# Gate and up tiles of three SwiGLU sublayers by seven half-size block products

## The chip, the core and the metric

One core of a Trainium2 chip runs the whole program. The metric is the device time of one execution in microseconds (us). TensorE (PE) multiplies; VectorE (DVE), ScalarE (ACT) and GpSimd (POOL) do the rest; SyncE (SP) issues the loads.

## The reference, cut to what matters

Two layers over 256 latent tokens and 256 context tokens with 1024 features. Each layer is an FFN sublayer, a mixer (a gated convolution in the first layer, windowed attention in the second) and another FFN sublayer. Each sublayer's input is normed and modulated by adaLN coefficients, which are products of silu(c) with a large projection w_mod.

```
def swiglu(h, w_gu, w_down):
    gu = h @ w_gu
    return (jax.nn.silu(gu[..., :D_FF]) * gu[..., D_FF:]) @ w_down

def ffn_sublayer(x, mod, k, g_pre, g_post, w_gu, w_down):
    h = adaln_in(x, g_pre, mod[k], mod[k + 1])
    return adaln_out(x, swiglu(h, w_gu, w_down), g_post, mod[k + 2], HALF_STEP)
```

D_FF is 2816, so w_gu has 22 feature tiles of 128 for the gate and 22 for up, each over 8 contraction tiles. Three FFN sublayers serve both token streams with the same weights; the fourth serves the latent stream alone.

## The kernel before

Everything lies with the features on the partitions: a stream is 8 tiles of 128 features by 512 tokens, the latent 256 (slice X) in front of the context 256 (slice Z). A float32 product is three float32r products: each operand is split into a high and a low part, and high x high, low x high and high x low are summed in PSUM (groups(), lines 398 to 400).

Weights come in slots of eight 128x128 tiles (512 KB). load() fetches a slot into a ring of RAW = 3 raw buffers, ACT writes its high part (line 243) and DVE, or POOL for the slots listed in POOL, its low part (line 244), into rings of RING = 8 buffers each. All loads are issued by SP in one order.

An FFN sublayer, ffn(l, j), is named by 3 * l + j: 0, 2 and 3 are the ones the change touches. Its 22 feature tiles go in three chunks (CHUNKS). A chunk first makes silu(gate) * up for its tiles, then multiplies them with the chunk's part of w_down into y, tile by tile of the output (project()). A tile of gate/up is one gate_up(): 48 matmuls of 512 columns, a silu on ACT (line 436), a product out of PSUM on DVE (line 438), and the split of the result (lines 408 and 409). In sublayers 2 and 3 the first four tiles are taken twice, for X and then for Z with 256 columns, so that the norms of the sublayer before can run beside them (HEADS, norms(), AT_HEAD); the end of a sublayer is halved in the same way (TAIL). In sublayer 0 the first two tiles run with the start.

Between these jobs pace() puts the adaLN sums: a step fetches one tile of w_mod (line 267) and takes the row sums of the one fetched before with silu(c), one DVE instruction per stream, called a dot here (line 297). NMODS says how many of the 18 chunks of eight steps are done by the end of sublayer 0, of the conv mixer and of sublayer 2; the rest go into sublayer 3. The last four chunks serve the latent stream alone.

The order of PE's instructions is that of the program. The other engines' order is made by a scheduler, except that instructions marked by keep() stay in the program's order. PSUM has four banks for products (bank()).

Of the kernel before, what the change touches and what calls it, by code (L numbers as in the profile page):

```python
# [18 lines left out]
F32 = mybir.dt.float32  # L19
# [13 lines left out]
CHUNKS = {0: ((0, 7), (7, 14), (14, 22)), 2: ((0, 7), (7, 14), (14, 22)), 3: ((0, 7), (7, 14), (14, 22))}  # L33
# [5 lines left out]
# feature tiles of the first two adaLN chunks: by dots, by pairs; and the loads ahead of the first product (latent  # L39
# and context stream, tiles for dots, tiles of pairs, weights)  # L40
# [4 lines left out]
RAW = 3  # L45
# [5 lines left out]
NMODS = (7, 6, 15)  # L51
# [15 lines left out]
# order in which the adaLN chunks are worked out: (layer, chunk, also for the context stream)  # L67
# [24 lines left out]
def halves_of(w):
    """[K, 1024] -> [K / 128, 128, 1024]: rows of two K tiles per slot, the front half of the columns first"""
    k = w.shape[0] // P
    return w.reshape(k // 2, 2, P, 2, 512).transpose(3, 0, 2, 1, 4).reshape(k, P, D)


def ffn_slots(w_gu, w_down, chunks):
# [3 lines left out]
    for a, b in chunks:  # L102
        out.append(slots_of(np.stack([gu[a:b], gu[FT + a:FT + b]], 1).reshape(-1, P, P)))
        out.append(slots_of(dn[:, a:b].reshape(-1, P, P)))
# [3 lines left out]
def lay_out(i):  # L108
    f = np.float32
    w = []  # L110
    w += ffn_slots(i["ffn_w_gu"][0, 0], i["ffn_w_down"][0, 0], CHUNKS[0])
    # the products of the first four slots run together, contraction tile by tile
# [4 lines left out]
    w += ffn_slots(i["ffn_w_gu"][0, 1], i["ffn_w_down"][0, 1], CHUNKS[2])  # L117
    w += ffn_slots(i["ffn_w_gu"][1, 0], i["ffn_w_down"][1, 0], CHUNKS[3])
# [6 lines left out]
    # the last sublayer keeps all of silu(gate) * up; its output comes with the tokens on the partitions  # L125
# [7 lines left out]
    # the first two chunks are taken together. Some of their feature tiles are worked out as the other chunks are;  # L133
    # the others go through the tensor engine, by pairs, with the rows of the projection on the partitions
# [10 lines left out]
    # constants of the shapes  # L145
# [26 lines left out]
# (half of the features, columns of it)  # L172
# [3 lines left out]
class Kernel:  # L176
    def __init__(self, ctx, tc, a):
# [40 lines left out]
        # silu(c), silu(c_ctx): on every partition, and with the features on the partitions  # L218
# [12 lines left out]
    # ---- streams of weights  # L231
    def load(self):
# [37 lines left out]
    def mod_step(self, last=False):  # L270
        """fetch one 128-feature tile of the adaLN projections, work out the one fetched before"""
# [22 lines left out]
    def dot(self, wt, v, b, out):  # L294
        """out = b + row sums of wt * silu(c)"""
# [3 lines left out]
    def keep(self, inst):  # L299
        """leave the marked instructions of an engine in the order of the program"""  # L300
# [24 lines left out]
    def spread(self, prb, r):  # L325
        """the same on all partitions, tokens along the row (PSUM)"""
# [7 lines left out]
    def new_h(self):  # L334
        """tiles of the modulated normed stream that the next product reads"""
# [41 lines left out]
    def weave(works, chain=None, at=()):  # L377
        """emit the works' products; the steps of chain go between them, at the given times (us of products)"""
# [41 lines left out]
    def gate_up(self, sl, base, ms, act):  # L420
        """silu(gate) * up of the feature tiles ms, whose products run together"""
# [11 lines left out]
        for i, m in enumerate(ms):  # L433
            pg, pu = banks[2 * i:2 * i + 2]
            sg = self.wk.tile([P, N], F32, name="sg", tag="tmp", bufs=3)
            nc.scalar.activation(sg[:, :n], pg[:, :n], AF.Silu)  # L436
            pr = self.wk.tile([P, N], F32, name="pr", tag="tmp", bufs=3)
            self.keep(nc.vector.tensor_mul(pr[:, :n], pu[:, :n], sg[:, :n]))  # L438
            self.hilo(act[m], sl, pr[:, :n], keep=True)

    def project(self, sl, base, ms, nk, act, y, part, fin=None):
        """y[m] (+)= W[:, m]^T act, for all of ms together; finished tiles are squared into the sums of fin and given
        their coefficients"""
# [651 lines left out]
```

## Time and profile before

| | us |
|---|---|
| median of 3 runs | 1680.61 |
| lowest and highest of the runs | 1678.48, 1683.15 |
| span of the profiled execution | 1676.8 |
| PE busy | 1642.4 |
| DVE busy | 1048.6 |
| ACT busy | 644.0 |
| POOL busy | 265.3 |

The profiled execution has no time of its own beside its span; the median of the runs lies 3.8 us above that. The span runs from the first to the last instruction. Busy times of different engines overlap. Matmuls are pipelined, so the time that one is shown with is longer than the step from one to the next; the step is read by counting matmuls in a stretch without waits.

### The profile page before, as it was taken

How to read it: one execution, taken by the hardware profiler on the slowest of the kernel's cores; microseconds unless marked ns; L12 is line 12 of the kernel's file. 1: busy time of each engine (PE TensorE's matmuls, PEld its weight loads, DVE VectorE, ACT ScalarE, POOL GpSimd, SP SyncE). 2: the span in 40 equal slices, each digit the busy share in tenths (PEclk: the TensorE clock that was granted, in tenths of full speed). 3: DMA queues.
4: the chain of work that ended last, by engine and by line, in shares of the span. 5: the costliest groups of instructions: out<-in, count | busy, mean ns of one | idle time of the engine just before them, and what ended most of it. 6: DMA issues, size and time to landing. Idle time of an engine off the chain costs nothing.

```text
span 1676.8 us, 23525 instructions
## 1 busy us (share of the span) xinstructions
PE 1642.4 (98%) x9378; PEld 1419.1 (85%) x9378; DVE 1048.6 (63%) x1570; ACT 644.0 (38%) x1051; POOL 265.3 (16%) x192
## 2 busy tenths in 40 slices
PE   8999999999999999999999999999999999989998
PEld 3788888889988998888888998888888997889987
DVE  7779779856644375977965564344443679665553
ACT  4532322325432643322232543222222558654442
POOL 1100000125102430000110521000000664130000
PEclk9999999999999999999999999999999999999999
DMA  8557556543322224655655224444433221045551
GB/s 317 188 164 237 189 187 217 194 156 102 101 89 101 68 71 165 213 188 165 219 191 166 80 74 148 160 132 150 153 124 114 94 89 64 26 160 198 194 192 50
DMA packets 70306, 246.73 MB, mean 147 GB/s; under 512 B 7730, under 2 KB 10290, under 8 KB 70196
## 3 DMA queue, kind: packets, MB, share of 16 engines
q1 hardware_dynamic: 69908, 245.02, 44.3%
q8 instruction: 73, 1.20, 0.3%
q14 instruction: 37, 0.30, 0.1%
q10 hardware_dynamic: 288, 0.20, 0.0%
HBM read 244.15 MB, written 1.05 MB: 146 GB/s over the span
## 4 chain that ended last, share of the span: by engine, by line
PE 90%; DVE 5%; ACT 2%; POOL 1%; issue 1%; DMA 1%; SPq 0%; DVEq 0%; POOLq 0%; ACTq 0%
PE mm L399 27%; PE mm L398 27%; PE mm L400 27%; PE mm L925 1%; PE mm L926 1%; PE mm L924 1%; PE po L801 1%; DVE junk L297 1%; PE tp L787 1%; POOL acc L359 1%; PE mm L747 1%; DMA xr<-in_xz 1%; PE prb L318 0%; ACT whi L243 0%; DVE acc L360 0%
## 5 line engine op out<-in xcount | busy, mean ns | idle before, releaser
L398 PE MATMUL mm<-hh,whi 128*128 128x512 f32 (+1 forms) x1520 | 549.3, 361 | 4.3 <-ACT hh L408 4.0
L399 PE MATMUL mm<-hh,wlo 128*128 128x512 f32 (+1 forms) x1520 | 547.9, 360 | 0.0
L400 PE MATMUL mm<-hl,whi 128*128 128x512 f32 (+1 forms) x1520 | 543.1, 357 | 0.0
L243 ACT ACTIVATE whi<-raw 128x1024 fp32r<-128x1024 f32 x316 | 330.5, 1056 | 440.2 <-PE mm L400 372.4
L244 DVE TENSOR_TENSOR wlo<-raw,whi 128x1024 fp32r<-128x1024 f32 x260 | 325.8, 1261 | 203.3 <-ACT whi L243 202.2
L398 PEld LDWEIGHTS mm<-hh,whi 128*128 128x128 f32 x1520 | 285.8, 188 | 53.6 <-ACT hh L408 5.3
L400 PEld LDWEIGHTS mm<-hl,whi 128*128 128x128 f32 x1520 | 285.9, 188 | 45.0 <-DVE hl L409 0.6
L399 PEld LDWEIGHTS mm<-hh,wlo 128*128 128x128 f32 x1520 | 286.3, 188 | 41.3
L297 DVE CUSTOM_DVE_ANT_0 junk<-wmd,sc,vec 128x1024 bf16<-128x1024 f32 x232 | 304.7, 1313 | 17.0 <-DMA wmd<-in_wmd 13.2
L244 POOL TENSOR_TENSOR wlo<-raw,whi 128x1024 fp32r<-128x1024 f32 x56 | 140.1, 2507 | 1005.2 <-ACT whi L243 1001.5
L398 PE MATMUL mm<-ah,whi 128*128 128x256 f32 (+1 forms) x848 | 276.8, 326 | 0.0
L399 PE MATMUL mm<-ah,wlo 128*128 128x256 f32 (+1 forms) x848 | 276.0, 326 | 0.0
L400 PE MATMUL mm<-al,whi 128*128 128x256 f32 (+1 forms) x848 | 274.1, 323 | 0.0
L398 PEld LDWEIGHTS mm<-ah,whi 128*128 128x128 f32 x848 | 160.5, 189 | 14.9
L400 PEld LDWEIGHTS mm<-al,whi 128*128 128x128 f32 x848 | 160.5, 189 | 14.1
L399 PEld LDWEIGHTS mm<-ah,wlo 128*128 128x128 f32 x848 | 160.8, 190 | 12.7
L438 DVE TENSOR_TENSOR pr<-mm,sg 128x512 f32<-128x512 f32 (+1 forms) x96 | 56.1, 584 | 181.6 <-PE mm L400 127.5
L436 ACT ACTIVATE sg<-mm 128x512 f32<-128x512 f32 (+1 forms) x96 | 49.2, 513 | 301.7 <-PE mm L400 301.7
L399 PE MATMUL mm<-h,wlo 128*128 128x256 f32 x352 | 98.8, 281 | 0.0
L398 PE MATMUL mm<-h,whi 128*128 128x256 f32 x352 | 98.6, 280 | 0.0
L400 PE MATMUL mm<-h,whi 128*128 128x256 f32 x352 | 98.4, 280 | 0.0
L409 DVE TENSOR_TENSOR al<-pr,ah 128x512 fp32r<-128x512 f32 (+1 forms) x84 | 74.6, 888 | 13.3 <-ACT ah L408 13.2
(185 smaller groups left out, 1496.5 us busy)
## 6 DMA issues: line engine op xcount, KB each, us to landing
raw<-in_wst SPq DMA_DIRECT2D x316, 512.0 KB, 3.5
wmd<-in_wmd SPq DMA_DIRECT2D x140, 512.0 KB, 4.2
xr<-in_xz SPq DMA_DIRECT2D x2, 1024.0 KB, 9.8
wmq<-in_wmd SPq DMA_DIRECT2D x8, 256.0 KB, 7.8
out_y<-xt SPq DMA_DIRECT2D x3, 256.0 KB, 2.1
rtab<-in_cst SPq DMA_DIRECT2D x1, 512.0 KB, 3.6
out_y<-xt SPq DMA_DIRECT2D x2, 128.0 KB, 1.8
msk<-in_cst ACTq DMA_DIRECT2D x1, 192.0 KB, 4.0
```

The costliest lines, as they stand in the source:

```text
L243: nc.scalar.activation(hi, raw, AF.Copy)
L244: d = sub.tensor_tensor(lo, raw, hi.bitcast(F32), ALU.subtract)
L297: self.keep(self.nc.vector.tensor_tensor_reduce(junk, wt, self.sc[v], 1.0, b, ALU.mult, ALU.add, out))
L359: nc.gpsimd.tensor_tensor(acc, acc, sq, ALU.add)
L398: nc.tensor.matmul(pt[:, :n], whi, rhi[:, sl], start=i == 0, stop=False)
L399: nc.tensor.matmul(pt[:, :n], wlo, rhi[:, sl], start=False, stop=False)
L400: nc.tensor.matmul(pt[:, :n], whi, rlo[:, sl], start=False, stop=i == last)
L409: i = (sub or self.nc.vector).tensor_tensor(lo[:, sl], src, hi[:, sl].bitcast(F32), ALU.subtract)
L436: nc.scalar.activation(sg[:, :n], pg[:, :n], AF.Silu)
L438: self.keep(nc.vector.tensor_mul(pr[:, :n], pu[:, :n], sg[:, :n]))
L747: nc.tensor.matmul(sp[e], act[4 * p2 + 2 * jp + jj][x][rows[e], qs], kt[p2][w][rows[e], :], start=a == 0, stop=False)
L787: nc.tensor.transpose(tp[:, c * P:(c + 1) * P], pe[c][:, kc // 2, kc % 2 * P:(kc % 2 + 1) * P], self.ident)
```

## The change

In sublayers 0, 2 and 3 the gate/up tiles from number SEVEN (6, 4 and 4) on are taken in pairs. The product of two feature tiles of gate and up with all 512 tokens is seen as a 2 x 2 block product: the weights in four blocks a11 (up, front half of the contraction), a21 (gate, front), a22 (gate, back) and a12 (up, back), each one slot; the input h in four blocks by the halves of the contraction and the two streams. Seven products of sums of blocks stand for the eight of the plain way (pair()): each is 24 matmuls of 256 columns, and PSUM banks gather several of them. The weights' sums are made on DVE for each pair; five of the seven low parts (POOLED) are on POOL. The sums of the inputs are made once per sublayer (forms()), before its first pair, in storage of y, of three of the eight buffers of each weight ring, and of the context halves of four tiles of h. There are 8, 9 and 9 pairs, and PE takes the seventh product of a pair behind the first of the next one.

The chunks are (0, 6), (6, 14), (14, 22). RAW is 6, the temporary tiles "tmp" have 4 buffers, not 3, and a smaller scratch for descriptors makes room. NMODS is (6, 8, 12), not (7, 6, 15): 32 steps in sublayer 0 (40 before), 16 in the conv mixer (0 before), 32 in sublayer 2 (64 before) and 48 in sublayer 3 (24 before). Comments are taken out.

```diff
-CHUNKS = {0: ((0, 7), (7, 14), (14, 22)), 2: ((0, 7), (7, 14), (14, 22)), 3: ((0, 7), (7, 14), (14, 22))}
+CHUNKS = {0: ((0, 6), (6, 14), (14, 22)), 2: ((0, 6), (6, 14), (14, 22)), 3: ((0, 6), (6, 14), (14, 22))}
+SEVEN = {0: 6, 2: 4, 3: 4}
+POOLED = (1, 2, 3, 4, 5)
-RAW = 3
+RAW = 6
-NMODS = (7, 6, 15)
+NMODS = (6, 8, 12)
...
-def ffn_slots(w_gu, w_down, chunks):
+def ffn_slots(w_gu, w_down, chunks, seven=FT):
     gu = tiles_of(w_gu)
     dn = tiles_of(w_down)
     out = []
     for a, b in chunks:
-        out.append(slots_of(np.stack([gu[a:b], gu[FT + a:FT + b]], 1).reshape(-1, P, P)))
+        c = min(max(a, seven), b)
+        if a < c:
+            out.append(slots_of(np.stack([gu[a:c], gu[FT + a:FT + c]], 1).reshape(-1, P, P)))
+        for m in range(c, b, 2):
+            for f, k in ((FT, 0), (0, 0), (0, 4), (FT, 4)):
+                out.append(slots_of(gu[f + m:f + m + 2, k:k + 4].reshape(-1, P, P)))
         out.append(slots_of(dn[:, a:b].reshape(-1, P, P)))
     return out
...
+    def raw(self, s):
+        assert s == self.slot_at, (s, self.slot_at)
+        self.slot_at += 1
+        raw = self.ring.tile([P, SLOT * P], F32, name="raw", tag="raw", bufs=RAW)
+        self.nc.sync.dma_start(out=raw, in_=self.a["wst"][s])
+        return raw
+    def split(self, src, sub=None):
+        hi = self.ring.tile([P, SLOT * P], F32R, name="whi", tag="whi")
+        lo = self.ring.tile([P, SLOT * P], F32R, name="wlo", tag="wlo")
+        self.nc.scalar.activation(hi, src, AF.Copy)
+        (sub or self.nc.vector).tensor_tensor(lo, src, hi.bitcast(F32), ALU.subtract)
+        return hi, lo
...
+    def forms(self):
+        nc, ring = self.nc, self.ring
+        hf = self.cp.tile([P, KT, N], F32, name="hf", tag="y")
+        for k in (4, 0, 5, 1, 6, 2, 7, 3):
+            hi, lo = (t.bitcast(F32) for t in self.h[k])
+            (nc.gpsimd if k % 4 in (1, 3) else nc.vector).tensor_tensor(hf[:, k], hi, lo, ALU.add)
+        fx, fz, bx, bz = (hf[:, k:k + 4, h] for k in (0, 4) for h in (X, Z))
+        tiles = [[ring.tile([P, 4, S], F32R, name="tf", tag=t) for t in ("whi", "wlo")] for _ in range(3)]
+        front = [[t[:, Z] for t in self.h[k]] for k in range(4)]
+        nc.vector.tensor_tensor(fx, fx, fz, ALU.subtract)
+        nc.vector.tensor_tensor(fz, bz, fz, ALU.subtract)
+        nc.scalar.activation(tiles[0][0], fz, AF.Copy)
+        nc.vector.tensor_tensor(tiles[0][1], fz, tiles[0][0].bitcast(F32), ALU.subtract)
+        nc.vector.scalar_tensor_tensor(bz, fx, -1.0, bz, ALU.mult, ALU.subtract)
+        nc.scalar.activation(tiles[1][0], bz, AF.Copy)
+        nc.vector.tensor_tensor(tiles[1][1], bz, tiles[1][0].bitcast(F32), ALU.subtract)
+        for k, (hi, lo) in enumerate(front):
+            nc.scalar.activation(hi, fx[:, k], AF.Copy)
+            nc.vector.tensor_tensor(lo, fx[:, k], hi.bitcast(F32), ALU.subtract)
+        nc.vector.scalar_tensor_tensor(bx, bz, -1.0, bx, ALU.mult, ALU.subtract)
+        nc.scalar.activation(tiles[2][0], bx, AF.Copy)
+        nc.vector.tensor_tensor(tiles[2][1], bx, tiles[2][0].bitcast(F32), ALU.subtract)
+        t3, t2, t4 = ([(hi[:, k], lo[:, k]) for k in range(4)] for hi, lo in tiles)
+        b11, b21, b22 = ([(hi[:, h], lo[:, h]) for hi, lo in self.h[k:k + 4]] for k, h in ((0, X), (4, X), (4, Z)))
+        return b11, t3, t2, b21, [tuple(f) for f in front], t4, b22
+    def pair(self, s, forms, act):
+        nc = self.nc
+        b11, t3, t2, b21, t1, t4, b22 = forms
+        gp = lambda i: nc.gpsimd if i in POOLED else None
+        def product(bank, w, rhs, first=False):
+            hi, lo = w
+            for m in range(2):
+                out = bank[:, m * S:(m + 1) * S]
+                for k in range(4):
+                    c = slice((4 * m + k) * P, (4 * m + k + 1) * P)
+                    rh, rl = rhs[k]
+                    mm = lambda w, r, start=False, stop=False: nc.tensor.matmul(out, w, r, start=start, stop=stop, skip_group_check=True)
+                    mm(hi[:, c], rh, start=first and m == 0 and k == 0)
+                    mm(lo[:, c], rh)
+                    mm(hi[:, c], rl, stop=k == 3)
+        tmp = lambda name, tag, **kw: self.wk.tile([P, N], F32, name=name, tag=tag, **kw)
+        a11 = self.raw(s)
+        w = self.split(a11, gp(0))
+        ba = self.bank()
+        product(ba, w, b11, True)
+        yield
+        up = tmp("up", "tmp", bufs=4)
+        nc.scalar.activation(up, ba, AF.Copy)
+        a21 = self.raw(s + 1)
+        s3 = self.ring.tile([P, SLOT * P], F32, name="raw", tag="raw", bufs=RAW)
+        nc.vector.tensor_add(s3, a11, a21)
+        w = self.split(s3, gp(1))
+        a22 = self.raw(s + 2)
+        nc.vector.tensor_add(a21, a21, a22)
+        bb = self.bank()
+        product(bb, w, t3, True)
+        gz = tmp("gz", "tmp", bufs=4)
+        nc.scalar.activation(gz, bb, AF.Copy)
+        nc.vector.tensor_add(a11, a21, a11)
+        w = self.split(a11, gp(2))
+        product(ba, w, t2)
+        gx = tmp("gx", "sq")
+        nc.scalar.activation(gx, ba, AF.Copy)
+        a12 = self.raw(s + 3)
+        w = self.split(a12, gp(3))
+        bc = self.bank()
+        product(bc, w, b21, True)
+        nc.vector.tensor_add(up, up, bc)
+        w = self.split(a21, gp(4))
+        product(ba, w, t1)
+        nc.vector.tensor_add(gz, gz, ba)
+        nc.scalar.activation(gz, gz, AF.Silu, scale=-1.0)
+        w = self.split(a22, gp(5))
+        product(bb, w, t4)
+        nc.vector.tensor_add(gx, gx, bb)
+        nc.scalar.activation(gx, gx, AF.Silu, scale=-1.0)
+        nc.vector.tensor_add(a12, a11, a12)
+        w = self.split(a12, gp(6))
+        yield
+        product(ba, w, b22)
+        nc.vector.tensor_mul(up, up, gx)
+        nc.vector.tensor_mul(gz, gz, ba)
+        for m in range(2):
+            c = slice(m * S, (m + 1) * S)
+            for t, h in ((up, X), (gz, Z)):
+                hi, lo = act[m]
+                nc.scalar.activation(hi[:, h], t[:, c], AF.Copy)
+                nc.vector.tensor_tensor(lo[:, h], t[:, c], hi[:, h].bitcast(F32), ALU.subtract)
...
+        forms = None
...
+            seven = SEVEN.get(3 * l + j, FT) - a
+            for m in range(m0, min(nk, seven)):
                 self.weave([self.gate_up(ALL, base, [m], act)])
                 pace(PACE)
+            if 3 * l + j in SEVEN and forms is None:
+                forms = self.forms()
+            last = None
+            for m in range(max(m0, seven), nk, 2):
+                p = self.pair(base + 2 * m, forms, act[m:m + 2])
+                next(p)
+                for _ in last or ():
+                    pass
+                next(p)
+                last = p
+                pace(2 * PACE)
+            for _ in last or ():
+                pass
             base += 2 * nk
             y = y if ci else self.new_y()
             part = ("first", "mid", "last")[ci]
             base += nk
...
```

## Rows read from the trace of the kernel before

**Rows 1.** The page: busy time by engine; slices; the chain; group of weights' high parts.
```profile
PE 1642.4 (98%) x9378; PEld 1419.1 (85%) x9378; DVE 1048.6 (63%) x1570; ACT 644.0 (38%) x1051; POOL 265.3 (16%) x192
...
PEclk9999999999999999999999999999999999999999
...
PE 90%; DVE 5%; ACT 2%; POOL 1%; issue 1%; DMA 1%; SPq 0%; DVEq 0%; POOLq 0%; ACTq 0%
...
L243 ACT ACTIVATE whi<-raw 128x1024 fp32r<-128x1024 f32 x316 | 330.5, 1056 | 440.2 <-PE mm L400 372.4
```

**Rows 2.** PE's waits: who waited for whom, us in total, times, longest.
```profile
PE prb L318 <- DVE acc L361: 9.6, 5, 2.7
...
PE prb L318 <- DVE cu L597: 0.2, 1, 0.2
```

**Rows 3.** Windows: a down stretch, a gate/up stretch, the last sublayer's gate/up.
```profile
core 0: us, PE busy (x) PEld busy (x) DVE busy (x) ACT busy (x) POOL busy (x), PEclk, DMA share, GB/s
669.85:708.30 38.45, 38.45 (x169) 31.55 (x168) 34.28 (x50) 12.03 (x15) 0.00 (x0) 1.00 0.67 215
708.30:785.00 76.70, 76.70 (x337) 62.92 (x336) 53.16 (x72) 21.84 (x28) 0.00 (x0) 1.00 0.56 180
1500.00:1600.00 100.00, 100.00 (x852) 100.00 (x851) 57.56 (x71) 47.43 (x73) 7.58 (x4) 1.00 0.60 199
```

**Rows 4.** Timeline of DVE and POOL, 311 to 319: start, duration, engine, line.
```profile
312.34 1.28 DVE L297 CUSTOM_DVE_ANT_0 junk<-wmd,sc,vec 128x1024 bf16<-128x1024 f32 x1
312.94 2.95 POOL L244 TENSOR_TENSOR wlo<-raw,whi 128x1024 fp32r<-128x1024 f32 x1 [8.58 <-ACT whi L243]
313.67 3.30 DVE L297 CUSTOM_DVE_ANT_0 junk<-wmd,sc,vec 128x1024 bf16<-128x1024 f32 x1
...
317.84 1.22 DVE L244 TENSOR_TENSOR wlo<-raw,whi 128x1024 fp32r<-128x1024 f32 x1 [0.26 <-ACT whi L243]
318.99 0.68 DVE L409 TENSOR_TENSOR al<-pr,ah 128x512 fp32r<-128x512 f32 x1
```

**Rows 5.** Timeline of POOL and DVE, 323 to 325 and 621 to 625.
```profile
323.98 2.40 POOL L244 TENSOR_TENSOR wlo<-raw,whi 128x1024 fp32r<-128x1024 f32 x1 [8.09 <-ACT whi L243]
...
621.25 2.42 POOL L244 TENSOR_TENSOR wlo<-raw,whi 128x1024 fp32r<-128x1024 f32 x1 [13.23 <-ACT whi L243]
622.14 2.60 DVE L244 TENSOR_TENSOR wlo<-raw,whi 128x1024 fp32r<-128x1024 f32 x1 [1.47 <-ACT whi L243]
```

**Rows 6.** Timeline of DVE and POOL in a tail, 393 to 397.
```profile
393.90 0.67 DVE L352 TENSOR_TENSOR xr<-xr,ut 128x512 f32<-128x512 f32 x1
394.50 0.41 DVE L459 TENSOR_TENSOR y<-y,mm 128x256 f32<-128x256 f32 x1
394.50 2.43 POOL L244 TENSOR_TENSOR wlo<-raw,whi 128x1024 fp32r<-128x1024 f32 x1
394.83 0.67 DVE L352 TENSOR_TENSOR xr<-xr,ut 128x512 f32<-128x512 f32 x1
```

**Rows 7.** Windows: the conv mixer's channels with both streams.
```profile
445.00:543.80 98.80, 98.80 (x434) 81.08 (x433) 44.72 (x52) 30.81 (x39) 12.13 (x5) 1.00 0.32 107
```

**Rows 8.** Windows: the context heads of sublayers 2 and 3.
```profile
613.50:636.80 23.30, 23.30 (x200) 23.30 (x200) 13.91 (x19) 10.34 (x19) 4.83 (x2) 1.00 0.34 111
984.70:1008.00 23.30, 23.30 (x200) 23.30 (x199) 13.47 (x20) 10.21 (x19) 6.83 (x3) 1.00 0.33 101
```

**Rows 9.** The norms' sums on POOL, line 359: duration ns min/median/max.
```profile
L359 POOL TENSOR_TENSOR acc<-acc,sq x16: 1277/1327/2318, 392.2 to 1346.8; 128x512 f32<-128x512 f32 x16
```

**Rows 10.** The waits of SP's queue, the longest in total.
```profile
SPq L238 <- DVE wlo L244: 783.3, 217, 28.6
SPq L267 <- DVE mod L297: 238.0, 117, 5.3
SPq L238 <- POOL wlo L244: 190.3, 44, 24.9
```

**Rows 11.** A wait of PE, and windows around it: PE busy, PEclk, DMA.
```profile
952.43 0.87 PE L318 MATMUL prb<-mean,acc 128*128 128x1 f32 x4 [1.98 <-DVE acc L361]
...
950.00:955.00 5.00, 3.02 (x17) 0.76 0.44 134
955.00:960.00 5.00, 5.00 (x41) 0.90 0.57 191
```

More of the change, by code (lines that the diff above doesn't have):

```diff
@@ L110, in lay_out @@
     w = []
-    w += ffn_slots(i["ffn_w_gu"][0, 0], i["ffn_w_down"][0, 0], CHUNKS[0])
+    w += ffn_slots(i["ffn_w_gu"][0, 0], i["ffn_w_down"][0, 0], CHUNKS[0], SEVEN[0])
     w[0][:4] = slots_of(w[0][:4].reshape(4, P, KT, P).transpose(2, 0, 1, 3).reshape(-1, P, P))
@@ L116, in lay_out @@
     w.append(slots_of(tiles_of(i["conv_w_out"][0]).reshape(-1, P, P)))
-    w += ffn_slots(i["ffn_w_gu"][0, 1], i["ffn_w_down"][0, 1], CHUNKS[2])
-    w += ffn_slots(i["ffn_w_gu"][1, 0], i["ffn_w_down"][1, 0], CHUNKS[3])
+    w += ffn_slots(i["ffn_w_gu"][0, 1], i["ffn_w_down"][0, 1], CHUNKS[2], SEVEN[2])
+    w += ffn_slots(i["ffn_w_gu"][1, 0], i["ffn_w_down"][1, 0], CHUNKS[3], SEVEN[3])
     qkv = i["attn_w_qkv"][0]
@@ L434, in gate_up @@
             pg, pu = banks[2 * i:2 * i + 2]
-            sg = self.wk.tile([P, N], F32, name="sg", tag="tmp", bufs=3)
+            sg = self.wk.tile([P, N], F32, name="sg", tag="tmp", bufs=4)
             nc.scalar.activation(sg[:, :n], pg[:, :n], AF.Silu)
-            pr = self.wk.tile([P, N], F32, name="pr", tag="tmp", bufs=3)
+            pr = self.wk.tile([P, N], F32, name="pr", tag="tmp", bufs=4)
             self.keep(nc.vector.tensor_mul(pr[:, :n], pu[:, :n], sg[:, :n]))
             self.hilo(act[m], sl, pr[:, :n], keep=True)
+    def forms(self):
[23 more added lines that the diff above has]
+        return b11, t3, t2, b21, [tuple(f) for f in front], t4, b22
@@ L515, in ffn @@
                     next(start, None)
-            for m in range(m0, nk):
+            seven = SEVEN.get(3 * l + j, FT) - a
+            for m in range(m0, min(nk, seven)):
                 self.weave([self.gate_up(ALL, base, [m], act)])
                 pace(PACE)
+            if 3 * l + j in SEVEN and forms is None:
[11 more added lines that the diff above has]
+                pass
             base += 2 * nk
@@ L593, in mix @@
             nh = n // S
-            cs = self.wk.tile([P, N], F32, name="sg", tag="tmp", bufs=3)
+            cs = self.wk.tile([P, N], F32, name="sg", tag="tmp", bufs=4)
             nc.scalar.activation(cs[:, :n], cg[:, :n], AF.Copy)
@@ L599, in mix @@
             nc.vector.tensor_mul(cu[:, :, 1:S + 1], v3(u), v3(cs))
-            t = self.wk.tile([P, N], F32, name="pr", tag="tmp", bufs=3)
+            t = self.wk.tile([P, N], F32, name="pr", tag="tmp", bufs=4)
             nc.scalar.activation(v3(t), cu[:, :, 0:S], AF.Identity, scale=self.cw(0, m))
@@ L639, in attention @@
         nc.scalar.dma_start(out=msk, in_=self.a["cst"][:, 4 * S:])
-        rot = wk.tile([P, P], F32, name="rot", tag="tmp", bufs=3)
+        rot = wk.tile([P, P], F32, name="rot", tag="tmp", bufs=4)
         nc.scalar.activation(rot, msk[:, 0:P], AF.Copy)
-        mib = wk.tile([P, 3 * P], BF16, name="mib", tag="tmp", bufs=3)
+        mib = wk.tile([P, 3 * P], BF16, name="mib", tag="tmp", bufs=4)
         mkb, idb = mib[:, :2 * P], mib[:, 2 * P:]
@@ L657, in rope @@
             else:
-                t, u = (lambda w: (w[:, 0], w[:, 1]))(wk.tile([P, 2, S], F32, name="t1", tag="tmp", bufs=3))
+                t, u = (lambda w: (w[:, 0], w[:, 1]))(wk.tile([P, 2, S], F32, name="t1", tag="tmp", bufs=4))
             nc.scalar.activation(t, p[:, X], AF.Copy)
@@ L1032, in turn @@
         def turn(p):
-            row = self.wk.tile([2, N], F32, name="row", tag="tmp", bufs=3)
+            row = self.wk.tile([2, N], F32, name="row", tag="tmp", bufs=4)
             nc.scalar.activation(row, sums[p][0:2, :], AF.Copy)
@@ L1089 @@
     arrays = lay_out({k: np.asarray(v) for k, v in inputs.items()})
-    nc = bacc.Bacc("TRN2", target_bir_lowering=False, num_devices=1)
+    nc = bacc.Bacc("TRN2", target_bir_lowering=False, num_devices=1, dynamic_dma_scratch_size=1024)
     build(nc, {n: v.shape for n, v in arrays.items()})
```

## The prediction

> **What bounds the kernel now.** I read the page's totals first, then the slices, then stretches of the stages, and last the instructions of VectorE (DVE) and GpSimd (POOL) one by one. TensorE (PE) is busy 1642.4 of 1676.8 us and the chain that ended last is 90% PE; DVE is busy for 63%, POOL for 16%, and PE's granted clock is in its top tenth in each slice [rows 1]. The fourteen lines of PE waits that the trace names (the first and the last are shown) sum to under 30 us, the largest 9.6 us behind a norm's sum [rows 2]. So only two things change the time: fewer TensorE columns, or work of another engine that becomes later than PE.
>
> A gate/up stretch runs 337 matmuls of 512 columns in 76.70 us, 228 ns each; the last sublayer runs 852 matmuls of 256 columns in 100 us, 117.4 ns each, with weight loads busy for all of it [rows 3]. DVE is busy 53.16 of the 76.70 us there, and 34.28 of 38.45 us in a down stretch: much less free than its 63% says.
>
> **The seven products.** Two feature tiles cost 2 x 2 x 8 x 3 = 96 matmuls of 512 columns now, 96 x 0.228 = 21.9 us. A pair by seven products is 7 x 2 x 4 x 3 = 168 matmuls of 256 columns; at the last sublayer's pace 168 x 0.1174 = 19.7 us. There are 8 + 9 + 9 = 26 pairs, so if PE never waits the change gives back 26 x 2.2 = 57 us. The ideal eighth would be 2.7 us a pair; the half-size matmul costs 51% of the full one, not 50%.
> The Trainium skill, "TensorE: Matmul & The Clock Gate", section "Back-to-back issue gap", gives an isolated spacing of columns over 2.4 GHz plus 2.5 ns: 215.8 and 109.2 ns. By it the gain would be 96 x 0.2158 - 168 x 0.1092 = 2.4 us a pair, 62 us in all; rows 3 have both spacings longer, and they decide.
>
> **What a pair asks of DVE and POOL.** Now two feature tiles need 4 splits of weights (low part 1.22 us each on DVE), 2 products out of PSUM and 2 low parts of 512. A pair needs four sums of weight blocks (s3, a21, a11, a12), seven low parts (five on POOL, the first and last on DVE), three sums and a product out of PSUM, one product in SBUF, and four low parts of 256 columns.
> How the two engines share is shown by every such meeting in the trace. A POOL low part alone takes 2.40 us [rows 5]. One that is issued during a DVE adaLN dot ends 2.27 us after that dot (313.62 to 315.89), and the next dot, issued beside it, takes 3.30 us, not 1.28; a DVE low part of weights issued beside one takes 2.60, not 1.22 [rows 4, 5]. So a DVE instruction with two SBUF operands and a POOL tensor_tensor run one after the other. Behind a DVE instruction that stands so are queued the weight sums (ScalarE's high parts wait for them, then PE) and the sums that free PSUM banks (PE waits for these directly). A DVE sum that reads PSUM keeps its 0.41 us beside POOL [rows 6].
> Steps from one DVE start to the next: 1.15 us for 1024 elements (317.84 to 318.99), 1.33 for a dot with its accumulator read (312.34 to 313.67) [rows 4], 0.60 for 512 elements and 0.33 for 256 [rows 6]. A pair's own DVE work is 6 x 1.15 + 0.60 (SBUF product) + 4 x 0.33 + 4 x 0.60 (PSUM) = 11.2 us. POOL takes 5 x 2.27 = 11.35 us in which DVE stands still, except where it happens to have a PSUM operation at its head. That overlap lies between 0 and 3.9 us (2.4 of PSUM operations, the rest gaps between instructions); I take 1.5, as about one DVE operation in five reads PSUM. So 11.2 + 11.35 - 1.5 = 21.05 us before any dot: already over PE's 19.7.
> The Trainium skill, "SBUF — State Buffer", section "Who interferes with whom", has this as a port that the loser waits for, with DVE operations of one SBUF input exempt. Its exemption used to the full (2.4 us) would take 0.9 us off each pair, 23 us off the sum; rows 4 to 6 agree with the exclusion, and no row shows so many such meetings in a line.
>
> **The adaLN dots.** pace() spreads them by jobs. First sublayer: 32 steps on 36 jobs, 2 jobs to a pair, 2 dots to a step: 3.56 dots, 4.7 us. Second FFN: 32 on 34, 3.76 dots, 5.0 us. Third: 48 on 34; its first 16 steps serve both streams, so the single pair has 5.65 dots (7.5 us), the second chunk's 3.3 (4.4), the third's 2.8 (3.75). A pair thus takes 25.8, 26.1, and 28.6, 25.4, 24.8 us, where now 21.9.
> The conv stage takes 16 steps: 32 x 1.33 = 42.6 us of DVE in a stretch of 98.8 us that has 44.7 [rows 7]. 87 of 98.8 fits, so I cost it at nothing; without that cover at most the excess, under 10 us.
>
> **What runs ahead.** Weights are split up to five slots ahead (eight, less three that the combined inputs hold), 5 x 2.84 = 14 us of products. But the seventh product overwrites the bank that the sum after the fifth reads, with only the sixth and the next pair's first between: 2 x 2.84 = 5.7 us. So DVE can trail PE by 5.7 to 14 us; I take 9, which a down stretch's spare DVE time can also supply: 43.9 us against 8 x 1.15 (splits) + 15 x 1.33 (dots) + 8 x 0.60 = 34.
>
> **The sum.** Six runs of four pairs (87.7 us each now): first sublayer 2 x (103.2 - 9 - 87.7) = +13.0; second 2 x (104.4 - 96.7) = +15.4; third (101.6 - 96.7) + (99.2 - 96.7) = +7.4. Two single pairs, without a head start since the combined inputs are made there: (26.1 - 21.9) + (28.6 - 21.9) = +10.9. forms() itself: four sums of 512 on DVE (2.4), four on POOL (1.33 each by the norm's sum of the same size [rows 9], 5.3), seven operations of 1024 on DVE (8.05) and four of 256 (1.3): 17 us. It must fit beside the context head, where DVE idles 9.4 and 9.8 of 23.3 us [rows 8], which hold part of the next tile's splits already: about 7 us late, twice, +14. In the first sublayer four full tiles run beside it: nothing. ScalarE gets seven high parts of 1.06 us [rows 1] and under 5 us of small ones a pair, and stays hidden. The weight DMAs stay four to a pair. RAW at 6 does not load further ahead than it seems: a pair's a11, a21, s3, a22 and a12 are held until their last sums. A weight DMA that waits for such a buffer stands in SP's queue ahead of the adaLN tiles, and SP waits already go mostly to low parts [rows 10]; that changes the order, not the bound.
> +13.0 + 15.4 + 7.4 + 10.9 + 14 = +61 us on a span of 1676.8: 1738. The three timed runs have their median 3.8 us above the span, so 1741; I say 1740.
>
> **Rivals.**
> (a) The lock's gaps are filled. Counting only what excludes: 5 x 2.27 + 6 x 1.08 (the blocked 1024 of rows 4 ends 1.08 us after POOL) + 0.54 + 4 x 0.27 (a half and quarters of it) = 19.5, and dots at 1.08: 23.6 us at most, with 14 us of lead. A run takes 94.2 - 14 = 80, against 87.7: 6 x 7.7 + 2 = 48 faster, so about 1632, or 1646 with forms() late. It wins over the forecast's sign below 23.4 us a pair: there six runs gain 6 x 3.1 = 19 and the rest costs 17. For it: DVE idles inside PE-bound stretches. Against: it needs DVE never to queue a second operation behind a blocked one, and its order is fixed.
> (b) PE alone sets the pace: 1680.6 - 57, about 1624. The combined inputs' splits would still be late. Rows 4 and 5 speak against it; it would need POOL and DVE to overlap.
> (c) Near break-even: pairs of 23.0 to 24.3 us, a lead of 9 and forms() late: 6 x (-4.7 to +0.5) + 2 x (1.1 to 2.4) + 14, so 1669 to 1702.
> (d) Slower still: the clock. Behind a wait of 1.98 us PE's granted clock was 0.76 of full over 5 us and 0.90 over the next 5 (1.2 GHz for a part of it): (0.24 + 0.10) x 5 = 1.7 us lost [rows 11]. Pairs that stand 4 to 6 us, some of it in one piece, would pay that: once in every pair +44, 1785. Without any overlap (26 x 1.5) and with a lead of 5.7 us (6 x 3.3), 1800; with both 1844. For it: PE has no such waits now, so its clock was never tried so. Against: waits spread over seven products are under 1 us each.
> That the products are not fewer is excluded by the code.
>
> **Chances.** Forecast (1700 to 1770) 0.60; (a) 0.13; (b) 0.05; (c) 0.10; (d) 0.12, mostly below 1800. About 0.3% (5 us) is what can be told from no change here. Faster: (a), (b) and a third of (c), 0.21; within: 0.04; slower: the rest, 0.75. The range 1655 to 1800 leaves out (b), most of (a) and the far end of (d).
>
> **What would show it.** Right: POOL busy near 570 us (265 + 130 x 2.41, less a few low parts that are pairs now); low parts and dots on DVE stretched to 2.3 to 3.5 us inside the pairs; PE idle in them, behind low parts of POOL or sums of DVE, 4 to 6 us a pair; a run of four pairs between two down stretches 92 to 98 us long; conv and the last sublayer as now. Wrong: PE gapless in the pairs at 117 ns (then b), or pairs of 20 to 22 us with DVE busy throughout (a). The prediction fails if DVE does its PSUM work inside POOL's time, or the dots move out of the pairs.

## The result and the profile after

The kernel after takes 1835.4 us (median; 1829.6 to 1836.5), the one before 1681.9 us beside it: a ratio of 1.0905, interval 1.0875 to 1.0934. The forecast was 1740 with a range up to 1800, so the direction came out and the size did not: +157 us on the spans (1676.8 to 1833.9) where +61 were forecast. The profiled execution of after took 1835.8 us.

The page of after, the lines that answer to [rows 1]: totals, clock by slice, the chain by engine, then the groups of POOL's low parts, of the adaLN dots and of a pair's matmuls.
```profile
PE 1655.5 (90%) x11250; PEld 1521.3 (83%) x11250; DVE 1430.0 (78%) x1805; ACT 778.4 (42%) x1280; POOL 637.8 (35%) x326
...
PEclk9899899898999999999998999989999999999999
...
PE 26%; DVE 9%; issue 4%; ACT 2%; DMA 2%; POOL 1%; DVEq 0%; ACTq 0%; POOLq 0%
...
L271 POOL TENSOR_TENSOR wlo<-raw,whi 128x1024 fp32r<-128x1024 f32 x130 | 371.7, 2876 | 555.3 <-ACT whi L270 459.3
L322 DVE CUSTOM_DVE_ANT_0 junk<-wmd,sc,vec 128x1024 bf16<-128x1024 f32 x232 | 403.6, 1740 | 11.1 <-DMA wmd<-in_wmd 8.6
L508 PE MATMUL mm<-hh,whi 128*128 128x256 f32 x832 | 254.5, 306 | 95.8 <-ACT gx L535 69.6
```
PE has 1872 instructions more and is busy almost as long as before, but for 90% of the span, not 98%; the traced chain is no longer PE's. A low part of a pair takes POOL 2.88 us on the mean, not 2.40, and a dot takes DVE 1.74. In the last line the time behind the bar is the reading: PE idled 95.8 us just ahead of these matmuls.

PE's waits in after (who waited for whom: us in total, times, longest). Before, the largest was 9.6 us behind a norm's sum [rows 2]; that wait is 9.3 us now.
```profile
PE mm L508 <- ACT gx L535: 69.6, 16, 7.1
PE mm L508 <- DVE gz L543: 26.2, 7, 7.1
PE mm L508 <- DVE wlo L271: 24.6, 9, 6.2
```
L508 is a pair's matmul, L535 ScalarE's copy of the third product out of PSUM (the fifth product goes into the same bank), L543 DVE's sum out of that bank after the fifth, L271 a low part. The 32 waits sum to 120 us. 20 of them are lumps of 3 to 7.1 us and make 107 us of this, a little under one lump to a pair.

Windows of after: the six runs of four pairs, then the two single pairs. The last line is of before, eight plain tiles that stood where a run of four pairs stands now.
```profile
core 0: us, PE busy (x) PEld busy (x) DVE busy (x) ACT busy (x) POOL busy (x), PEclk, DMA share, GB/s
145.00:260.60 115.60, 89.72 (x673) 88.27 (x673) 113.91 (x119) 42.83 (x60) 51.18 (x17) 0.87 0.48 156
306.00:422.60 116.60, 89.75 (x674) 88.11 (x673) 114.03 (x117) 45.49 (x63) 58.92 (x20) 0.87 0.47 153
770.80:865.00 94.20, 84.82 (x674) 84.13 (x673) 78.86 (x71) 42.72 (x61) 46.21 (x17) 0.95 0.42 129
908.90:1015.90 107.00, 87.98 (x673) 86.92 (x673) 99.54 (x95) 45.27 (x63) 50.95 (x18) 0.90 0.47 152
1188.50:1290.20 101.70, 85.58 (x673) 84.30 (x673) 92.59 (x88) 42.74 (x61) 48.46 (x17) 0.93 0.50 164
1334.20:1435.50 101.30, 87.82 (x673) 86.77 (x672) 92.69 (x84) 45.04 (x63) 51.02 (x18) 0.92 0.56 182
702.00:729.80 27.80, 23.11 (x171) 22.70 (x170) 26.89 (x30) 10.93 (x14) 8.30 (x4) 0.89 0.51 186
1119.60:1150.20 30.60, 22.73 (x170) 22.32 (x169) 30.04 (x28) 11.27 (x15) 20.55 (x8) 0.89 0.47 167
272.60:360.30 87.70, 87.70 (x385) 71.95 (x384) 67.18 (x92) 24.70 (x31) 16.57 (x6) 1.00 0.59 192
```
From a run's first product to its last these are 115.4, 116.5, 94.0, 106.8, 101.5 and 101.3 us: 635.5, where six times 87.7 stood. In sublayer 0 DVE is busy 98 to 99% of the time; in the other runs it has 1.9 to 3.8 us a pair left. Where the 157 us are:

| | us |
|---|---|
| six runs of four pairs (635.5 against 526) | +109.5 |
| two single pairs (27.6 and 30.5 against 21.9 each) | +14.3 |
| first down stretches, three (33.9, 40.7, 38.0 against 32.9) | +13.9 |
| gate/up heads of sublayers 2 and 3 (49.3, 50.8 against 46.5) | +7 |
| attention (156.3 against 150.1), start about +3, the rest | +12.5 |

One stall, in the timeline of after (start, duration, engine, line; in brackets the idle time before it and its releaser; instructions in between left out).
```profile
206.19 9.48 POOL L271 TENSOR_TENSOR wlo<-raw,whi 128x1024 fp32r<-128x1024 f32 x3
207.24 2.88 DVE L553 TENSOR_TENSOR up<-up,gx 128x512 f32<-128x512 f32 x1
210.04 3.42 DVE L322 CUSTOM_DVE_ANT_0 junk<-wmd,sc,vec 128x1024 bf16<-128x1024 f32 x1
...
214.00 2.76 DVE L322 CUSTOM_DVE_ANT_0 junk<-wmd,sc,vec 128x1024 bf16<-128x1024 f32 x1
...
217.36 1.21 DVE L549 TENSOR_TENSOR raw<-raw 128x1024 f32<-128x1024 f32 x1
...
218.60 1.06 ACT L270 ACTIVATE whi<-raw 128x1024 fp32r<-128x1024 f32 x1 [3.29 <-DVE raw L549]
...
219.57 0.58 ACT L535 ACTIVATE gx<-mm 128x512 f32<-128x512 f32 x1
...
220.20 0.58 PE L508 MATMUL mm<-hh,whi 128*128 128x256 f32 x1 [7.13 <-ACT gx L535]
```
Read it from the end. PE waits 7.13 us for a copy of 0.58 us, whose input had long been there. The copy stood in ScalarE's queue behind the high part of a weight sum; that sum (L549) came on DVE only at 217.36, after a 512-element product of 2.88 us and two dots of 3.42 and 2.76, all three stretched by POOL's three low parts in a row. So in this stall the exclusion of [rows 4, 5] reaches PE through ScalarE's order. No run moved this copy alone, so what the order costs by itself stays open.

Windows of after around the end of that stall (columns as above).
```profile
215.00:220.00 5.00, 0.00 (x0) 0.00 (x0) 5.00 (x8) 1.71 (x3) 0.67 (x1) 0.51 0.35 95
220.00:225.00 5.00, 4.80 (x22) 4.80 (x23) 5.00 (x7) 2.15 (x3) 2.19 (x1) 0.50 0.86 273
225.00:230.00 5.00, 5.00 (x43) 5.00 (x42) 5.00 (x4) 0.00 (x0) 1.16 (x1) 0.97 0.64 234
```
PE did nothing from 215 to 220, and its granted clock fell to 0.51; once it ran again, it had 22 matmuls done in 5 us at 1.2 GHz, and 43 in the next 5. Over all, the clock stood at its lower level for 185 us of the span, against 21 before.

### The profile page after: what moved, and what is told of

It reads as the page before. It is cut to its first block, busy times and chain, and to the rows that moved or that the text cites. A ratio compares the mean times of both kernels' runs of the same rounds, so it can differ in the third digit from the quotient of the medians.

```text
span 1833.9 us, 27992 instructions
## 1 busy us (share of the span) xinstructions
PE 1655.5 (90%) x11250; PEld 1521.3 (83%) x11250; DVE 1430.0 (78%) x1805; ACT 778.4 (42%) x1280; POOL 637.8 (35%) x326
## 5 line engine op out<-in xcount | busy, mean ns | idle before, releaser
L271 POOL TENSOR_TENSOR wlo<-raw,whi 128x1024 fp32r<-128x1024 f32 x130 | 371.7, 2876 | 555.3 <-ACT whi L270 459.3
L322 DVE CUSTOM_DVE_ANT_0 junk<-wmd,sc,vec 128x1024 bf16<-128x1024 f32 x232 | 403.6, 1740 | 11.1 <-DMA wmd<-in_wmd 8.6
L508 PE MATMUL mm<-hh,whi 128*128 128x256 f32 x832 | 254.5, 306 | 95.8 <-ACT gx L535 69.6
L423 PE MATMUL mm<-ah,whi 128*128 128x256 f32 (+1 forms) x848 | 277.9, 328 | 2.2 <-ACT ah L559 2.2
L508 PE MATMUL mm<-hh,wlo 128*128 128x256 f32 x832 | 252.4, 303 | 25.3 <-DVE wlo L271 24.6
L508 PEld LDWEIGHTS mm<-hh,whi 128*128 128x128 f32 x832 | 175.6, 211 | 100.7 <-ACT gx L535 72.9
L508 PE MATMUL mm<-hl,whi 128*128 128x256 f32 x832 | 250.3, 301 | 0.0
L508 PE MATMUL mm<-tf,whi 128*128 128x256 f32 x1248 | 236.3, 285 | 2.1 <-ACT up L520 2.1
L423 PE MATMUL mm<-hh,whi 128*128 128x256 f32 (+1 forms) x688 | 225.7, 328 | 5.3 <-ACT hh L433 5.0
L425 PE MATMUL mm<-hl,whi 128*128 128x256 f32 (+1 forms) x688 | 222.8, 324 | 5.1 <-DVE hl L398 3.9
L424 PE MATMUL mm<-hh,wlo 128*128 128x256 f32 (+1 forms) x688 | 221.9, 322 | 0.0
L508 PEld LDWEIGHTS mm<-tf,whi 128*128 128x128 f32 x1248 | 201.2, 194 | 2.3 <-ACT up L520 2.3
L508 PEld LDWEIGHTS mm<-hh,wlo 128*128 128x128 f32 x832 | 175.9, 211 | 28.3 <-DVE wlo L271 26.5
L254 POOL TENSOR_TENSOR wlo<-raw,whi 128x1024 fp32r<-128x1024 f32 x48 | 121.9, 2545 | 221.1 <-ACT whi L253 215.3
L508 PE MATMUL mm<-tf,wlo 128*128 128x256 f32 x624 | 177.9, 285 | 0.0
L423 PEld LDWEIGHTS mm<-ah,whi 128*128 128x128 f32 x848 | 162.0, 191 | 17.1 <-ACT ah L559 2.9
```

The costliest lines, as they stand in the source:

```text
L254: d = sub.tensor_tensor(lo, raw, hi.bitcast(F32), ALU.subtract)
L271: (sub or self.nc.vector).tensor_tensor(lo, src, hi.bitcast(F32), ALU.subtract)
L322: self.keep(self.nc.vector.tensor_tensor_reduce(junk, wt, self.sc[v], 1.0, b, ALU.mult, ALU.add, out))
L423: nc.tensor.matmul(pt[:, :n], whi, rhi[:, sl], start=i == 0, stop=False)
L424: nc.tensor.matmul(pt[:, :n], wlo, rhi[:, sl], start=False, stop=False)
L425: nc.tensor.matmul(pt[:, :n], whi, rlo[:, sl], start=False, stop=i == last)
```

## The experiments

Theories. **Lock** (X, where the expectations use letters): a POOL low part and a DVE operation with two SBUF inputs run one after the other, and the five low parts on POOL are what makes a pair dear. **Load** (Y): DVE has too much to do, wherever the low parts are, the dots first of all. **Edits**: forms(), the chunks, the buffers, the new places of the dots cost it.

### Plain tiles with all other edits
```
-SEVEN = {0: 6, 2: 4, 3: 4}
+SEVEN = {}
```


> No pairs and no combined inputs; the chunks, RAW, buffers and the new spread of the adaLN sums stay. Both theories: these cost nothing, 1676 to 1690 us, as the kernel before. If the spread of the adaLN sums over the stages is itself dear (32 dots in the conv mixer), over 1700 us.

Measured 1685.5 us, ratio 1.0033 (1.0018 to 1.0048). Chunks of 6, 8 and 8, six buffers and the new spread of the dots cost 0.3%: the 157 us come with the pairs and their combined inputs.

### No low part of a pair on POOL
```
-POOLED = (1, 2, 3, 4, 5)
+POOLED = ()
```


> All seven low parts of a pair on DVE, none on POOL. Theory X (POOL's low parts and DVE's two-operand instructions exclude each other, so both add up in one chain): a pair's chain falls from 11.2 + 11.35 - 1.5 = 21 us to 11 x 1.15 + 0.6 + 1.3 + 2.4 = 17 us beside the dots; with the 4.8 dots that a pair has on average in the changed kernel's trace (116 in 24 pairs) 23.4 us, runs of four pairs near 94 us instead of 94 to 117, the whole near 1760 us. Rival Y (DVE's own load and the order of its queue are the trouble, and POOL relieves it): 5 x 1.15 = 5.8 us more DVE work in each of 26 pairs, so slower than 1835 us, up to 1980.

Measured 1715.2 us, ratio 1.0200 (1.0176 to 1.0224): 120 us less than after, by giving DVE more work, and 45 us below the number of X itself; it is still 2% slower than before. The runs take 87.3, 85.4, 79.7, 84.1, 82.7 and 84.2 us. PE's waits in this kernel:
```profile
PE mm L508 <- DVE wlo L271: 15.8, 7, 3.4
PE mm L423 <- ACT ah L559: 13.8, 5, 4.2
```
The copy L535 no longer appears. The first product of the down stretch (L423) now waits: the dots that DVE did not get done in the pairs come there (49.5 us for 43.7 in sublayer 0, and its tail 67.8 for 47.8).

### Three low parts on POOL
```
+POOLED = (1, 3, 5)
```


> Low parts 1, 3 and 5 of a pair on POOL, 2 and 4 on DVE. Theory X (each low part on POOL is added to DVE's chain): on the line between none on POOL (1715 us) and five (1835 us): 1787 us. Rival W (POOL is harmful only as one long chain of four dependent low parts, 1 to 4): most of the loss gone, 1740 us or less.

Measured 1786.3 us, ratio 1.0629 (1.0607 to 1.0651), as X had it. With 0, 3 and 5 low parts on POOL: 1715, 1786, 1835 us. That is 24 us for each of a pair's low parts that POOL has, 24 / 26 = 0.92 us a pair; the exclusive time of POOL less what DVE then saves, 2.27 - 1.15 = 1.12 us [rows 4], was a little more.

### ScalarE writes the low parts' tiles
```
+        if sub: self.nc.scalar.activation(lo, src, AF.Copy)
```
The five tiles hold a copy, not the low part. 

> The five low parts of a pair that POOL makes are written by ScalarE instead, as a plain copy of the weights (so not the low part): no POOL work in the pairs, no more DVE work. Theory X: DVE has 11.2 + 4.8 x 1.33 = 17.6 us a pair, PE 19.7: runs of four pairs 79 to 85 us, the whole 1660 to 1690 us. Rival Y (the order of the queues, not POOL): ScalarE's queue gets 5 us longer a pair, so no gain, 1800 us or more.

Measured 1676.0 us, ratio 0.9967 (0.9951 to 0.9983), with every dot in its place. The runs take 80.9, 84.9, 79.7, 79.6, 79.6 and 79.6 us. With POOL's low parts off both engines the pairs run at PE's pace: four of six runs show it, and a fifth is 1.3 us off. The rest is not free: two first down stretches of 41.2 and 42.9 us, heads of 49.4 and 50.4, so that 42 us gained in the runs leave 4 on the span.

### Without the dots
```
-        nc.vector.tensor_tensor_reduce(junk, wt, self.sc[v], ...)
+        nc.vector.tensor_tensor_reduce(junk[:, :64], wt[:, :64], self.sc[v][:, :64], ...)
```
The dots run over 64 of 1024 columns. First with the low parts on POOL as in after: 

> The adaLN dots take 64 of 1024 columns (the rest of those sums is left out), all else as in the changed kernel. Theory X: the chain keeps 21 us a pair, PE is nearly the bound: runs of four pairs near 86 us, the whole near 1715 us (some of it also from places outside the pairs). Rival Y: the order of the dots in DVE's queue is the whole trouble, so PE's pace, 79 us a run, and 1630 to 1650 us.

Measured 1750.8 us, ratio 1.0412 (1.0387 to 1.0437). Neither number was met. Two of its runs, in windows, then the second of them for the dots alone (columns: DVE's dots, PEclk, DMA), then its largest wait:
```profile
141.80:242.00 100.20, 86.58 (x673) 85.55 (x672) 78.89 (x105) 43.01 (x61) 44.99 (x17) 0.93 0.51 166
...
727.60:812.60 85.00, 81.78 (x673) 81.34 (x672) 63.84 (x54) 42.94 (x61) 45.27 (x17) 0.98 0.39 116
```
```profile
727.60:812.60 85.00, 0.00 (x0) 0.98 0.39 116
```
```profile
PE mm L508 <- ACT gx L535: 45.1, 17, 5.1
```
DVE idles 21 us in each of these runs and PE waits all the same, at the same copy. The second run has no dot in it at all and takes 85.0 us, 5.4 us more than with no low part on POOL (79.6, next experiment): that much POOL's low parts cost a run by themselves, and with DVE idle for a quarter of it, not as load. The other five runs take 94.0 to 100.2 us with 7 to 26 short dots each. The short dots are not free. Those in the runs keep DVE busy for 60.8 us, 0.69 us each on the mean where the median of all is 0.285, because one that meets a low part waits for it (the longest took 2.5 us). And for 5 to 12 us of such a run DVE stands idle until a dot's tile of w_mod has landed. So this experiment takes the dots' length out, but not their turns or their place in DVE's order. That the lumps come from the order that POOL, DVE, ScalarE and PE each keep fits these rows; no run changed that order alone.

Then with POOLED = () besides: 

> All low parts on DVE and the dots over 64 of 1024 columns (the rest of those sums is left out): DVE has 17.6 us a pair, PE 19.9, nothing on POOL. Theory X: all runs of four at PE's own 79.6 us, the whole 1640 to 1660 us; what is missing to 1624 us is the price of the combined inputs at the heads and of the first chunk. Rival (lumps of waits come from the form of the pair itself, its PSUM banks and ScalarE's queue): runs of 84 us or more, 1680 us or more.

Measured 1661.3 us, ratio 0.9890 (0.9870 to 0.9911), just above X's range. Now runs of 79.6, 79.6, 79.7, 79.6, 81.0 and 79.6 us. The four kernels together, six runs of four pairs, us (before: 526):

| | whole dots | short dots | the length costs |
|---|---|---|---|
| five low parts on POOL | 635.5 | 568.4 | 67 |
| all on DVE | 503.4 | 479.1 | 24 |
| POOL costs | 132 | 89 | |

Both theories hold, POOL's part is the larger, and 43 us appear only with both. The scheduler did not put as many dots into the runs of all four (116 and 98 whole ones, 88 and 89 short ones), so part of each difference is their place. And even with DVE idle for a third of the span and the runs at PE's pace the span falls by 21 us alone: the runs and single pairs take 50 us less than before, and 28 of these go to heads, first down stretches (35.8 and 39.7), tails, attention and the start.

### The dots in conv
```
-NMODS = (6, 8, 12)
+NMODS = (4, 8, 12)
```


> The changed kernel with NMODS = (4, 8, 12): 16 steps (32 dots) go from sublayer 0 to the conv mixer, as the prediction had taken them to. Theory X (pairs are bound by DVE's chain with POOL in it): the two runs of pairs of sublayer 0 (115.4 and 116.5 us) come down to those of sublayer 2 (94.0 and 106.8), the conv mixer stays at 98.6 us: 31 us less, 1804 us, at the least 1793 (32 x 1.33 = 43). Rival Z (the spread of the sums costs nothing where they are): 1835 us.

Measured 1819.5 us, ratio 1.0831 (1.0797 to 1.0865). Sublayer 0's runs fall to 101.5 and 104.8 us (-25.6) and the conv stretch stays at 98.8, but its head, which had none, has 13 dots and takes 45.7 us, not 35.8. About 16 us of the gain are left: less than the theory said, more than the rival.

### Can pairs pay?
All of these have POOLED = (). Three sublayers from tile 6 on, the dots weighted towards the down stretches (PACE), and the pair's two last products held in the written order:
```
+POOLED = (); SEVEN = {0: 6, 2: 6, 3: 6}; NMODS = (6, 8, 12); PACE = 0.5
+        self.keep(nc.vector.tensor_mul(up, up, gx)); self.keep(nc.vector.tensor_mul(gz, gz, ba))
```


> All low parts on DVE, the pair's two products kept in DVE's program order with the dots, pairs from tile 6 on in all three sublayers (two plain tiles beside the combined inputs), dots at half weight beside gate/up jobs (PACE 0.5). NMODS as in the changed kernel. Theory X: a pair asks DVE for 17.0 + 2.6 to 3.8 dots = 20.4 to 22 us; 24 pairs at PE's 19.9 us would give 1680 - 50; with what the first low-on-DVE kernel loses in its down stretches mended, 1640 to 1665 us. Rival (plain tiles in the first chunk do not help and half-size products lose elsewhere): 1690 us or more.

Measured 1727.2 us, ratio 1.0281 (1.0256 to 1.0305). The same with NMODS = (4, 8, 12), PACE = 0.25: 

> As the kernel before this one, with NMODS = (4, 8, 12) (32 dots in the conv mixer) and the dots at a quarter of the weight beside gate/up jobs (PACE 0.25): 1.6 dots a pair, DVE 19.1 us of PE's 19.9. Theory X: runs of four pairs at 79.6 to 81 us, 1635 to 1655 us. If the down stretches, which get 3 dots a job, become late: 1665 us or more.

Measured 1709.3 us, ratio 1.0180 (1.0152 to 1.0208). Both are misses, on the rival's side, and one wait of the second shows one reason.
```profile
1146.26 0.58 PE L508 MATMUL mm<-tf,whi 128*128 128x256 f32 x1 [27.95 <-ACT up L520]
```
A copy behind a product that is held in order: 28 us at once, in a run of 109.4 us; three such waits sum to 51 us in the first. Ahead of that product DVE took seven dots in a row, and four of them waited for their tile of w_mod. Holding the order made a new wait. Without it, NMODS = (5, 8, 12), PACE = 0.5: 

> All low parts on DVE, pairs in all three sublayers from tile 6 on (24 pairs), NMODS = (5, 8, 12), PACE 0.5, no added order. Theory X: sublayer 0 has 80 dots, 3.1 a pair, DVE 21.1 us of PE's 19.9: its runs 84 to 88 us, those of sublayers 2 and 3 80 to 84; 1670 to 1685 us, no better than the kernel before. Rival (DVE's load is not what is left): below 1660 us.

Measured 1706.3 us, ratio 1.0167 (1.0148 to 1.0185): runs of 86.8, 89.2, 84.3, 84.3, 85.8 and 82.8. That is above both numbers, so a miss again; the waits behind the held product are gone, and the runs are still 3 to 10 us longer than PE's pace. The reading, not tested further: three sublayers have more dots than their holes take. Two, with SEVEN = {2: 6, 3: 6} and NMODS = (7, 10, 13): 

> A version that is to beat both: all low parts on DVE, pairs in sublayers 2 and 3 alone and from tile 6 on (16 pairs), sublayer 0 with plain tiles and 112 dots as in the kernel before, 16 dots in the conv mixer, NMODS = (7, 10, 13), PACE 0.5, no added order. Theory X: DVE 17.0 + 1.6 to 1.9 dots = 19.1 to 19.6 us a pair, PE 19.9: four runs of 80 to 82 us for 87.7, so 23 to 31 us off 1680, less what the combined inputs cost in heads and tails (about 12 us by the earlier runs): 1660 to 1672 us. Rival (the heads, tails and the first chunk take all of it back): 1676 us or more.

Measured 1680.7 us, ratio 1.0002 (0.9988 to 1.0016), a miss on the rival's side. Its four runs are at 79.7 to 81.1 us, as the theory had it; but a plain run of sublayer 0 has 92.7 us for 87.7 (4.5 of them PE's waits behind a tile's silu and product, L461 and L463), and conv's head, into which 13 dots came, 46.0 for 36.4. So, last, the sublayer with the fewest dots alone, the other two and their dots as before:
```
+POOLED = (); SEVEN = {3: 6}; NMODS = (7, 6, 15); CHUNKS 0 and 2 as before
```


> Only the sublayer with the fewest adaLN dots takes pairs (sublayer 3: 24 steps for one stream, so 24 dots), all low parts of the pairs on DVE; sublayers 0 and 2, their chunks and all adaLN steps are as in the kernel before. Theory (pairs pay where DVE has room: 17 us of its own per pair against 19.9 of PE, with under 2 dots a pair): runs of four pairs of 80 to 81 us where 87.7 stood, Z head about 3 us longer, down of chunk 0 less than 1 us longer; sublayer 3 from 324.4 to about 312, net -9, so 1668 to 1674 us against 1680. Rival (what two sublayers gave back came from the pairs themselves, through forms(), heads and first down stretches, not from the dots that were moved into sublayer 0 and conv): 1677 or more.

Measured 1674.3 us, ratio 0.9959 (0.9946 to 0.9972): 0.3 us above the theory's range and below the rival's. Its two runs, in windows:
```profile
1075.00:1155.00 80.00, 80.00 (x674) 79.96 (x673) 65.40 (x75) 44.10 (x61) 0.00 (x0) 1.00 0.46 143
1199.00:1278.70 79.70, 79.70 (x673) 79.69 (x672) 72.04 (x88) 46.33 (x63) 2.42 (x1) 1.00 0.58 183
```
PE without a gap, at full clock, DVE with 2 to 4 us a pair to spare. Sublayer 3 goes from 324.4 to 309 us, the tail and head before it give back 7, and the start takes 5 more. Of the kernels that leave nothing out it is the only one under the time of before, by 0.4%.

## Why the prediction was wrong, step by step

**Held.** A pair that never waits: 19.7 us were worked out, 19.9 measured (79.6 for four). The exclusion of POOL and DVE as the largest part of the loss: the experiment without POOL's low parts alone gives back 120 of the 157 us, and the dose of three lies between. It does not decide the sign alone, since that kernel is still 2% slower than before. POOL's busy time came to 638 us, not 570, because a low part took 2.88 us. The single pairs and forms(), roughly: +24.9 forecast; single pairs, first down stretches and heads measured +35. The prediction had forms() late beside the heads, and most of it came in the first down stretches.

**Failed: the dots of sublayer 0 and conv.** "32 steps on 36 jobs" is wrong, and so is what stands ahead of the prediction on it. pacer() is set up before start() sets the first step's number, so sublayer 0 is given 48 steps (it had 56 before, and sublayer 2 had 48), and conv none; the third FFN sublayer's share was right. The windows of the runs, DVE's dots alone (line L322), with the conv stretch last:
```profile
core 0: us, DVE busy (x), PEclk, DMA share, GB/s
145.00:260.60 115.60, 56.30 (x32) 0.87 0.48 156
306.00:422.60 116.60, 55.57 (x30) 0.87 0.47 153
770.80:865.00 94.20, 11.19 (x7) 0.95 0.42 129
908.90:1015.90 107.00, 35.67 (x18) 0.90 0.47 152
1188.50:1290.20 101.70, 26.91 (x16) 0.93 0.50 164
1334.20:1435.50 101.30, 25.24 (x13) 0.92 0.56 182
474.00:573.00 99.00, 0.00 (x0) 1.00 0.31 99
```
62 dots in the two runs of sublayer 0, where eight pairs at 3.56 make 28; 116 in all six where the prediction's counts make 83. The 48 steps put 42 into these two runs, and the kernel with no low part on POOL has 44 there. The others came by DVE's order: the program puts 12, 20 and 22 dots beside the plain tiles and the first two down stretches of sublayer 0, and the trace has 6, 15 and 16 there. At the prediction's 1.33 us the 33 are worth 44 us. Measured, they are worth less: the experiment that moved steps to conv took 28 dots out of these two runs and 25.6 us, 0.91 us each. The trace of before could have told the step count: it has 100 dots from 118.8 to 445 us, where 40 steps make 80 in the whole sublayer.

**Failed: the lead of 9 us a run.** By the prediction's formula with the dots that were really there the six runs are 24 x 21.05 + 116 x 1.33 = 659.5 us; they took 635.5, so the lead was 24 us, not 54: 11 and 8 in sublayer 0, 4 or less in the others. These 30 us and the dots' 44 are the 74 by which the runs missed (+109.5 for +35.8). That PE has no such lead shows without dots, too: the run with none took 85.0 us, where 84.2 less a lead of 9 would have left PE's own 79.6. But the formula fits better than its reasons hold, and that is in part luck. In the run with no dot DVE is busy for 63.8 us, not 84.2, so the 85.0 are not DVE's work; and a dot costs 0.58 us by its length (67 / 116) or 0.91 by its removal, not 1.33. The formula lacks the waits in order, and it charges dots that fill the holes these waits leave. The bound of 5.7 us in the prediction named the right bank (L535, L543); that ScalarE's copy out of it stands behind a high part, which stands behind DVE, was not seen.

**Rival (d), the clock, was nearest** (1785 to 1844), and what was said against it was wrong: the waits are not spread over seven products but come as lumps of 3 to 7 us, and behind 19 of the 20 PE works for 3 to 6 us at 1.2 GHz. Counted along PE, all pairs take 693.7 us in after: 517.7 at PE's own pace, 123.3 in waits, and 52.8 that are left, most of them the lower clock: outside the waits it stood at 1.2 GHz for 97 us of the pairs, which loses 48. Before they took 570.4. What the clock alone is worth at the end stays open: where DVE is busy 99% (sublayer 0), a faster PE would only wait more, and no run changed the clock by itself.

**Rivals (a) to (c).** (a) and (c) needed pairs of at most 23.6 and 24.3 us; one run of after has 23.5, with 7 dots in it, the others 25.3 to 29.1. (b) came true only where POOL had no low part of a pair.

**Costed at nothing, wrongly.** Attention, start and the rest: +12.5 us, not taken apart. The clock, which the sum left to a rival: the 48 us above. With plain tiles and the other edits unchanged the heads keep 46.4 us, so the 7 us there belong to the pairs and their combined inputs; which operation does it was not taken apart.

## What to carry to other kernels

Before work is moved to GpSimd, count on VectorE's lane what both do with two SBUF inputs: here a low part on GpSimd cost 0.92 us a pair more than the same on VectorE, with GpSimd 65% idle. When a stretch becomes bound by an engine next to TensorE, look for the smallest instruction that TensorE waits for and what stands ahead of it in its queue: the wait comes in one piece, and the clock falls behind it. And take the number of spread-out operations in a stretch from the trace, never from the loop that spreads them.

## What was not expected of the hardware

Even a very small DVE operation pays the full turn. Timeline of after, DVE and POOL:
```profile
175.47 8.64 POOL L271 TENSOR_TENSOR wlo<-raw,whi 128x1024 fp32r<-128x1024 f32 x3
176.52 2.36 DVE L314 SCALAR_TENSOR_TENSOR mod<-mod,vec 128x8 f32<-128x8 f32 x1
...
179.40 2.37 DVE L314 SCALAR_TENSOR_TENSOR mod<-mod,vec 128x8 f32<-128x8 f32 x1
```
Two sums of eight elements took 2.36 and 2.37 us; the median of the nine is 0.161. The Trainium skill, "SBUF — State Buffer", section "Who interferes with whom", says that the loser of the shared port is blocked for the whole of the other's instruction, whatever its own shape; these two rows agree with it.
